# The low part of every third weight chunk from an accumulating DMA, in a two-layer fp32 decoder trunk

## The chip, the cores and the metric

The kernel runs on one core of a Trainium2 chip. The metric is the device time of one execution in microseconds (us). Three runs of the kernel before gave 1068.85, 1066.88 and 1071.05 us, median 1068.85. The core has five engines that work side by side, each through its own list of instructions in order: TensorE (PE, matmul, with its weight loads as PEld), VectorE (DVE), ScalarE (ACT), GpSimd (POOL) and SyncE (SP, which here only issues DMAs). DMAs run on 16 DMA engines that all queues share.

## The reference

One sequence of 512 tokens, width 1024, all in float32, goes through two layers. Layer 0 mixes tokens with sliding-window attention, layer 1 with a chunked spatial gating unit (SGU); each mixer is followed by a SwiGLU feed-forward (FFN) of inner width 2816. Every weight matrix is used once.

```python
def swiglu(h, w_gate_up, w_down):
    gu = h @ w_gate_up
    return (jax.nn.silu(gu[..., :D_FF]) * gu[..., D_FF:]) @ w_down

def chunked_sgu(h, w_in, ln_g, ln_b, w_spatial, b_spatial, w_out):
    z = jax.nn.gelu(h @ w_in)
    u, v = z[..., :SGU_WIDTH], z[..., SGU_WIDTH:]
    v = layernorm(v, ln_g, ln_b)
    ...
    mixed = jnp.einsum('gts,bnsgd->bntgd', ws, vg) + b_spatial.T[None, None, :, :, None]
    return (u * mixed) @ w_out          # reshapes left out

# every layer:
x += rmsnorm(mixer(rmsnorm(x)));  x += rmsnorm(swiglu(rmsnorm(x)))
```

## The kernel before, in words

**Products.** A float32 product is made from three products of a shorter type, fp32r: each operand is held as a high part (the value copied to fp32r) and a low part (the value minus its high part), and `mm3` issues high·high, high·low and low·high into one accumulator. For activations the parts are `hh`/`hl` (normed input), `ga`/`gb` (FFN inner), `rt`/`ga` (SGU output); for weights they are `wh`/`wl`.

**Weight stream.** The weights lie in memory as 1408 blocks of 128x128 in the order of their use, grouped in 176 chunks of 8 blocks (128 x 1024 floats, 512 KB). Chunks 0 to 19 belong to attention, 20 to 85 to the first FFN, 86 to 109 to the SGU (86 to 89 and 92 to 95 its `v` half, 90, 91 and 96 to 101 its `u` half, 102 to 109 its output projection), 110 to 175 to the second FFN. `fetch()` issues a chunk's load on SP into one of two `raw` buffers (line 232). `split()` then makes the parts: ACT copies `raw` into `wh` (line 255), and the inner generator `low()` has DVE subtract, `wl = raw - wh` (line 251; for chunks 0 and 1 POOL does it, line 248). Behind the subtraction `low()` calls `fetch()` for the chunk two further on, which takes the same `raw` buffer. `wh` and `wl` take one slot each of a pool of 17 slots, and a slot comes free when TensorE has used the chunk's last block. Five to eight split chunks wait ahead of TensorE in long matmul stretches.

**Order of the work.** Nothing is reordered by hand: the program that writes the kernel keeps an estimated clock for each engine (`now` for TensorE, `busy["v"]` for DVE, `busy["a"]` for ACT, `busy["d"]` for loads), advances it with every instruction it writes, and holds side chains (`Side`: norms, evacuations, splits) each with a due time. Whenever a clock passes a due time, the chain's next step is written. `split_idle()` decides when the next chunk's split is written, from the estimated idle time of DVE and ACT and a table `PLAN` per stage; `blk()` makes TensorE's order wait, at writing time, for `chunks[c][3]`, the estimated end of the chunk's low part. So the order of instructions on every engine follows from the estimates, and what they are for one instruction moves others. On the chip only the order and the data dependences count.

**Norms between stages.** A token tile's norm needs squares on ACT (line 368), a short DVE chain for the reciprocal root (`rstd`, lines 351 to 374), a scaled copy of `x` (`m`, ACT line 412 and DVE line 415), transposes on TensorE into `aux` (line 446), and evacuations into `hh` (ACT, line 459) and `hl` (DVE, line 463). Tiles 0 and 1 go together, and 2 and 3. While the norm of tiles 2 and 3 runs, TensorE works on the columns of tiles 0 and 1 of the next stage (256-column matmuls).

Of the kernel before, what the change touches and what calls it, by code (L numbers as in the profile page):

```python
# [6 lines left out]
F32 = mybir.dt.float32  # L7
I32 = mybir.dt.int32
F32R = mybir.dt.float32r
AF = mybir.ActivationFunctionType  # L10
ALU = mybir.AluOpType
PSUM = bass.MemoryType.PSUM

P = 128
# [8 lines left out]
CB = 8  # L23
# [8 lines left out]
NRAW = 2  # L32
PLAN = [(10.0, 0.0, 1.2, (), (2,)), (6.0, 0.8, 0.0, (3,), (1, 2)), (2.0, 0.3, 1.2, (2, 3), (2,)), (8.0, 0.8, 1.2, (2, 3), (2,)), (6.0, 0.3, 1.2, (2, 3), (2,)), (5.0, 0.3, 1.6, (2, 3), (2, 3)), (10.0, 0.3, 1.2, (2, 3), (2, 3)), (6.0, 0.3, 1.2, (2, 3), (2,))]
LAT = 0.1
DLAT = 1.7
X_0 = 4.0
RS = (0.27406385, -4.2420223, 5.2654107, -0.90349173, 1.7067959)
# [17 lines left out]
GU0 = WO1 + 32  # L55
# [8 lines left out]


def uses(i):
    """How many products of a 128 x 128 block the tensor engine makes with different token tiles."""
    if i < Q0 or WO0 <= i < GU0 or SO0 <= i < GU1:
        return 4
    if SV0 <= i < SO0:  # L70
        return 4 if i < SU0 or SV1 <= i < SU1 else 2 if i < SV1 else 1
    if i < WO0:
        return 1
    b = i - GU0 if i < SV0 else i - GU1
    f, b = divmod(b, 3 * HJ * KT)
    if b >= 2 * HJ * KT:
        return 4
    return 2 if f == 0 and b < 3 * 2 * KT else 1
# [3 lines left out]
def trunk_kernel(ctx, tc, x_t, w, cols, rows, ws_t, consts, out):  # L82
    nc = tc.nc
# [7 lines left out]
    wp = pool("wp", NW)  # L91
# [7 lines left out]
    def nm(s):  # L99
        cnt[0] += 1  # L100
        return f"{s}_{cnt[0]}"
# [21 lines left out]
    cols2 = [slice(0, S), slice(S, D)]  # L123
    full = slice(0, S)

    # ---- order of issue: every engine runs in the order of this trace; a clock per engine estimates
    # ---- when work is done, and a side chain joins the trace when its next step can run
    now = [0.0]
    busy = {"v": 0.0, "a": 0.0, "d": 0.0, "p": 0.0}
    sides = []  # L130

    def V(n, ready, fixed=0.07):
        busy["v"] = max(busy["v"], ready) + fixed + n * 0.00104
        return busy["v"] + LAT

    def A(n, ready, fixed=0.09):
        busy["a"] = max(busy["a"], ready) + fixed + n * 0.00084
        return busy["a"] + LAT

# [19 lines left out]
            elif not split_idle():  # L159
                return  # L160

    # the tensor engine runs at half its clock until it has been busy for a while
    zero = tp.tile([P, 4 * S], F32, tag="p", name="zero", bufs=NP)[:, 0:128].bitcast(mybir.dt.bfloat16)
    nc.vector.memset(zero[:], 0.0)
    idle_ps = [None]
# [19 lines left out]
            if not f():  # L185
                pass_time(max(now[0] + 0.01, first().due))

    # slots whose last use is traced by a side chain
    slots = {"rt": 3, "t": NT, "acc": 6}

    def take(tag):
# [20 lines left out]
        mm(ps, ah, bl, False, False)  # L212
        mm(ps, al, bh, False, stop)

# [1 line left out]
    NCH = NBLK // CB  # L216
    raws, chunks = {}, {}
    used, cur, hold, pace = [0], [0], [0.0], [5.1]
# [17 lines left out]
    def split():  # L236
        c = len(chunks)
        fetch()
        raw, ready = raws[c]
        assert used[0] + 2 <= NW  # L240
        used[0] += 2
        wh = wp.tile([P, CB * P], F32R, tag="w", name=nm("wh"))
        wl = wp.tile([P, CB * P], F32R, tag="w", name=nm("wl"))

        def low(f):
            yield f
            if c in POOL_LOW:
                nc.gpsimd.tensor_tensor(wl[:], raw[:], wh[:].bitcast(F32), ALU.subtract)
                chunks[c][3] = f + 2.4
            else:  # L250
                nc.vector.tensor_tensor(wl[:], raw[:], wh[:].bitcast(F32), ALU.subtract)  # L251
                chunks[c][3] = V(CB * P, f)
            fetch(chunks[c][3])

        nc.scalar.activation(wh[:], raw[:], AF.Copy)  # L255
        f = A(CB * P, ready)
        chunks[c] = [wh, wl, None, None, f]
        chunks[c][2] = Side(low(f), f)
# [49 lines left out]
    def drop(n=1):  # L308
        used[0] -= n

# [1 line left out]
    xs = [xp.tile([P, D], F32, tag=f"x{k}", name=f"x{k}") for k in range(NB)]  # L312
    c_cols = cp.tile([P, 42], F32, name="c_cols")
    c_msk = cp.tile([P, 384], F32, name="c_msk")
# [27 lines left out]
    def b_qk(i):  # L342
        return c_cols[:, 32 + i:33 + i]

# [1 line left out]
    def rsqrt(us, ready, scale=1.0):  # L346
        ws = [[small(1, i) for i in ("vt", "vy", "vz", "vq", "vw")] for _ in us]
        rs = [sp.tile([P, 8], F32, tag="rc", name=nm("rc"), bufs=8)[:, 0:1] for _ in us]
# [171 lines left out]
                self.nx.add(t, s2, self.m, f)  # L520

    class LastTok(Tok):
        """The last token tile: nothing runs behind it, so its second half comes in two pieces."""
        parts = (slice(0, S), slice(S, S + 256), slice(S + 256, D))

        def __init__(self, t, m, g1, spare_m):
# [65 lines left out]
            if free:  # L592
                give("acc")

# [1 line left out]
    def ffn(base, nx_in, g1o, nx_out):  # L596
        def evac_gu(g, jj, pg, pu, hf):
            n = hf.stop - hf.start
# [100 lines left out]
                    toks[t].add(i + 1, ps, V(256, now[0] + 0.2))  # L699
            drop()  # L700

# [1 line left out]
    def attention(nx_in, g1o, nx_out):  # L703
        v4 = wp.tile([P, NB, 256], F32, tag="w", name=nm("vt"))
        vt = [v4[:, t] for t in range(NB)]
# [4 lines left out]
        ready = {}  # L710
# [105 lines left out]
        def softmax(u, g2, st, es, sm, f):  # L816
# [13 lines left out]
            V(4, f, 0.15)  # L830
            f = busy["v"] + LAT
            for j in js[NA:]:
# [8 lines left out]
        def values(u):  # L841
# [11 lines left out]
            fs = {}  # L853

            def pv(kt):
                """Both heads of a pair, side by side in the columns of the array."""
                f = max(fs[2 * kt], fs[2 * kt + 1])
                if f > now[0]:
                    yield f
                for i in range(2):  # L860
                    o = (2 * pr + i) * 64
                    nc.tensor.matmul(po[i * 64:i * 64 + 64, :], vt[n - nkt + 1 + kt][:, o:o + 64], todo[2 * kt + i],  # L862
                                     start=kt == 0, stop=kt == nkt - 1)
                    now[0] += 0.02 if i else 0.86
                    give("t")
# [19 lines left out]
            f = A(S, now[0] + 0.2)  # L885
# [14 lines left out]
        order = []  # L900
# [64 lines left out]
            hold[0] = now[0] + (NB - 1 - t) * 8 * 0.65  # L965
        drop(2)

# [1 line left out]
    def sgu(nx_in, g1o, nx_out):  # L969
        ln_g, ln_b, bsp = row_tile(0), row_tile(1), row_tile(2)  # L970
        h = hsrc(nx_in)
# [279 lines left out]
```

## Time and profile before

| | us |
|---|---|
| runs | 1068.85, 1066.88, 1071.05 (median 1068.85) |
| span of the profiled execution | 1067.4 |
| median less span | 1.45 |
| PE busy | 1047.9 (98% of the span) |
| DVE busy | 524.6 (49%) |
| ACT busy | 439.8 (41%) |
| POOL busy | 23.6 (2%) |
| mean granted TensorE clock | 0.997 of full speed (2.4 GHz) |

The trace comes from one profiled execution, whose span runs from its first to its last instruction; a busy share is an average over stages, so what counts at a place is read from the rows of that place. A row of the timeline has the start, the duration, engine, line, operation, destination `<-` sources and, in brackets, how long the engine stood idle before it and what ended that. `xN` is a run of N equal instructions put in one row, with their time together. Matmuls overlap, so a matmul's duration is longer than the distance to the next one's start; the distance is what it costs.

### The profile page before, as it was taken

How to read it: one execution, taken by the hardware profiler on the slowest of the kernel's cores; microseconds unless marked ns; L12 is line 12 of the kernel's file. 1: busy time of each engine (PE TensorE's matmuls, PEld its weight loads, DVE VectorE, ACT ScalarE, POOL GpSimd, SP SyncE). 2: the span in 40 equal slices, each digit the busy share in tenths (PEclk: the TensorE clock that was granted, in tenths of full speed). 3: DMA queues.
4: the chain of work that ended last, by engine and by line, in shares of the span. 5: the costliest groups of instructions: out<-in, count | busy, mean ns of one | idle time of the engine just before them, and what ended most of it. 6: DMA issues, size and time to landing. Idle time of an engine off the chain costs nothing.

```text
span 1067.4 us, 13460 instructions
## 1 busy us (share of the span) xinstructions
PE 1047.9 (98%) x5288; PEld 873.5 (82%) x5288; DVE 524.6 (49%) x1103; ACT 439.8 (41%) x792; POOL 23.6 (2%) x21
## 2 busy tenths in 40 slices
PE   7999998999999999999999999999999999999997
PEld 6877766988888888888888888899888888888886
DVE  7588879743332233332474867584333223333335
ACT  6589776632322223232255343573223222232210
POOL 2000001000000000000000000100000000000000
PEclk9999999999999999999999999999999999999999
DMA  5322201332222222224132232033222222222202
GB/s 206 126 79 80 80 21 60 134 125 98 99 99 98 99 99 99 98 84 136 60 117 101 80 125 103 30 119 147 92 98 99 99 99 99 99 99 99 99 0 79
DMA packets 29263, 103.00 MB, mean 96 GB/s; under 512 B 3280, under 2 KB 3808, under 8 KB 29200
## 3 DMA queue, kind: packets, MB, share of 16 engines
q1 hardware_dynamic: 28512, 101.00, 26.1%
q8 instruction: 41, 0.67, 0.2%
q10 hardware_dynamic: 576, 0.92, 0.2%
q0 software_dynamic: 112, 0.23, 0.2%
q14 instruction: 22, 0.18, 0.0%
HBM read 100.04 MB, written 2.10 MB: 96 GB/s over the span
## 4 chain that ended last, share of the span: by engine, by line
PE 92%; DVE 4%; DMA 2%; ACT 1%; issue 1%; SPq 0%; DVEq 0%; ACTq 0%
PE acc L204 88%; PE acc L862 1%; PE aux L870 1%; DMA x<-x_t 1%; DMA raw<-w 1%; DVE wl L251 1%; PE aux L446 1%; DVE x L509 0%; DVE u L374 0%; DVE hl L463 0%; DVE m L963 0%; DVE p L833 0%; DVE m L1141 0%; PE acc L446 0%; DVE vt L353 0%
## 5 line engine op out<-in xcount | busy, mean ns | idle before, releaser
L251 DVE TENSOR_TENSOR wl<-raw,wh 128x1024 fp32r<-128x1024 f32 x174 | 213.5, 1228 | 415.9 <-PE acc L204 341.4
L204 PE MATMUL acc<-hh,wh 128*128 128x512 f32 (+1 forms) x960 | 351.7, 366 | 0.0
L204 PE MATMUL acc<-hl,wh 128*128 128x512 f32 (+1 forms) x960 | 349.9, 364 | 0.6 <-DVE hl L463 0.6
L204 PE MATMUL acc<-hh,wl 128*128 128x512 f32 (+1 forms) x960 | 349.7, 364 | 0.0
L255 ACT ACTIVATE wh<-raw 128x1024 fp32r<-128x1024 f32 x176 | 185.8, 1057 | 221.9 <-PE acc L204 187.8
L204 PE MATMUL acc<-wh,ga 128*128 128x512 f32 (+1 forms) x736 | 234.6, 389 | 3.0 <-DVE ga L889 3.0
L204 PEld LDWEIGHTS acc<-hl,wh 128*128 128x128 f32 x960 | 181.1, 189 | 29.4 <-DVE hl L463 1.0
L204 PEld LDWEIGHTS acc<-hh,wh 128*128 128x128 f32 x960 | 181.1, 189 | 28.9
L204 PEld LDWEIGHTS acc<-hh,wl 128*128 128x128 f32 x960 | 181.0, 189 | 28.9
L204 PEld LDWEIGHTS acc<-wh,ga 128*128 128x128 f32 x736 | 137.2, 188 | 35.2 <-DVE ga L889 3.4
L204 PE MATMUL acc<-wl,ga 128*128 128x512 f32 (+1 forms) x368 | 141.7, 385 | 0.0
L601 ACT ACTIVATE t<-acc 128x512 f32<-128x512 f32 (+1 forms) x50 | 27.2, 544 | 146.9 <-PE acc L204 146.9
L204 PEld LDWEIGHTS acc<-wl,ga 128*128 128x128 f32 x368 | 69.2, 188 | 12.7
L204 PE MATMUL acc<-wh,gb 128*128 128x512 f32 (+1 forms) x198 | 61.9, 383 | 0.0
L611 ACT ACTIVATE ga<-t 128x512 fp32r<-128x512 f32 (+1 forms) x38 | 21.4, 563 | 53.2 <-DVE t L607 53.1
L204 PEld LDWEIGHTS acc<-wh,gb 128*128 128x128 f32 x198 | 36.9, 188 | 7.2
L490 POOL TENSOR_TENSOR m<-m,row 128x512 f32<-128x512 f32 x12 | 16.9, 1409 | 1020.4 <-ACT acc L368 1020.4
L204 PE MATMUL acc<-wl,gb 128*128 128x512 f32 (+1 forms) x99 | 37.9, 383 | 0.0
L368 ACT ACTIVATE acc<-m 128x512 f32<-128x512 f32 x30 | 17.9, 598 | 45.4 <-DVE m L676 42.1
L204 PE MATMUL acc<-wh,hh 128*128 128x512 f32 (+1 forms) x96 | 34.6, 363 | 1.5 <-ACT wh L255 1.5
L204 PE MATMUL acc<-wl,hh 128*128 128x512 f32 (+1 forms) x96 | 34.0, 364 | 0.0
L204 PE MATMUL acc<-wh,hl 128*128 128x512 f32 (+1 forms) x96 | 33.9, 355 | 0.0
(117 smaller groups left out, 838.9 us busy)
## 6 DMA issues: line engine op xcount, KB each, us to landing
raw<-w SPq DMA_DIRECT2D x176, 512.0 KB, 3.4
row<-rows SPq DMA_DIRECT2D x8, 512.0 KB, 4.6
x<-x_t SPq DMA_DIRECT2D x4, 512.0 KB, 5.6
out<-x SPq DMA_DIRECT2D x4, 256.0 KB, 2.1
out<-x ACTq DMA_DIRECT2D x3, 256.0 KB, 2.1
cs<-consts SPq DMA_DIRECT2D x1, 512.0 KB, 4.7
t<-ws_t SPq DMA_DIRECT2D x2, 256.0 KB, 4.5
c_row<-rows POOLq DMA_DIRECT2D x1, 136.0 KB, 7.3
```

What stands on the lines that cost most here:

```text
L204: nc.tensor.matmul(ps, a, b, start=start, stop=stop)
L251: nc.vector.tensor_tensor(wl[:], raw[:], wh[:].bitcast(F32), ALU.subtract)
L255: nc.scalar.activation(wh[:], raw[:], AF.Copy)
L368: nc.scalar.activation(junk, src, AF.Square, accum_out=s[:, c:c + 1])
L446: nc.tensor.transpose(dst, self.src[t][k // 4][:, (k % 4) * P:(k % 4 + 1) * P], ident)
L490: nc.gpsimd.tensor_tensor(self.m[c][:], self.m[c][:], self.g1[:, cols2[c]], ALU.mult)
L601: nc.scalar.activation(t1[:, hf], pg[:, hf], AF.Silu)
L611: nc.scalar.activation(g[0][jj][:, hf], t1[:, hf], AF.Copy)
L862: nc.tensor.matmul(po[i * 64:i * 64 + 64, :], vt[n - nkt + 1 + kt][:, o:o + 64], todo[2 * kt + i], start=kt == 0, stop=kt == nkt - 1)
L870: nc.tensor.transpose(pT[:, g * P:(g + 1) * P], u.pt[:, g, i, kt * P:(kt + 1) * P], ident)
```

## The change

Behind attention, from chunk 28 on, the chunks whose number is a multiple of 3 (30, 33, ..., 174: 49 chunks) get their low part in another way. ACT writes `wh` as before, and then a second copy with scale -1, `-wh`, into the slot of the low part (now called `wlq`). An accumulating DMA issued by POOL then adds `raw` onto it: -wh + raw. DVE has no part in these chunks. The load of the chunk two further on takes the same `raw` buffer, and so comes behind the accumulating DMA. The estimate of that DMA's length, `DMA_LOW`, is 6.0 us. Comments and docstrings are gone too; they are not shown here. Line numbers behind the new code are 21 higher than before (`wl` on DVE is line 272, the plain `wh` 276, the squares 389, the scaled copy 433, the transposes 467).

```diff
+DMA_LOW = 6.0
...
+    def by_dma(c):
+        return c * CB >= GU0 + 64 and c % 3 == 0
+
     NCH = NBLK // CB
...
         wh = wp.tile([P, CB * P], F32R, tag="w", name=nm("wh"))
+        if by_dma(c):
+            wl = wp.tile([P, CB * P], F32R, tag="w", name=nm("wlq"))
+
+            def low_dma(f):
+                yield f
+                nc.scalar.activation(wl[:], wh[:].bitcast(F32), AF.Copy, scale=-1.0)
+                f = A(CB * P, f)
+                yield f
+                nc.gpsimd.dma_start(wl[:], raw[:], accum_op=ALU.add)
+                chunks[c][3] = f + DMA_LOW
+                fetch(chunks[c][3])
+
+            nc.scalar.activation(wh[:], raw[:], AF.Copy)
+            f = A(CB * P, ready)
+            chunks[c] = [wh, wl, None, None, f]
+            chunks[c][2] = Side(low_dma(f), f)
+            return
         wl = wp.tile([P, CB * P], F32R, tag="w", name=nm("wl"))
```

DVE has 49 instructions fewer, ACT 49 more, POOL 49 DMAs more; PE and SP have as many as before. Because the estimates differ, the order moves as well, at the changes of stage above all. Three places follow; names end in a number that the program counts up, and `...` stands for rows left out.

The first is TensorE at the start of the SGU, where the transposes of the last two token tiles of FFN 0 (`aux<-c_id,m`) are mixed into the 256-column matmuls on chunk 90 (`wh_789`, `wl_790`; in the change `wlq_790`) and chunk 91 (`wh_802`). Before:

```order
L204 MATMUL acc_822_4856<-hh_747_4610,wh_789_4751 128x256
L204 MATMUL acc_822_4856<-hl_755_4618,wh_789_4751 128x256
L204 MATMUL acc_822_4856<-hh_747_4610,wl_790_4752 128x256
...
L204 MATMUL acc_822_4856<-hh_754_4617,wl_790_4752 128x256
L204 MATMUL acc_825_4886<-hh_747_4610,wh_802_4791 128x256
...
L204 MATMUL acc_825_4886<-hh_748_4611,wl_803_4792 128x256
L446 MATMUL aux_826_4893<-c_id_96,m_541_3139 128x128
L446 MATMUL aux_826_4893<-c_id_96,m_543_3141 128x128
```

In the change:

```order
L205 MATMUL acc_820_4874<-hh_747_4630,wh_789_4771 128x256
L205 MATMUL acc_820_4874<-hl_755_4639,wh_789_4771 128x256
L205 MATMUL acc_820_4874<-hh_747_4630,wlq_790_4772 128x256
L467 MATMUL aux_821_4878<-c_id_96,m_541_3146 128x128
L467 MATMUL aux_821_4878<-c_id_96,m_543_3148 128x128
...
L205 MATMUL acc_820_4874<-hh_748_4631,wh_789_4771 128x256
```

The first transpose stood behind 30 of these matmuls (24 on chunk 90, 6 on chunk 91) and now stands behind 3, so it moved ahead of 27.

The second is ACT at the same place: the splits of chunks 90 and 91, the squares of tile 3 (`m_543,s2<-x3`) and the scaled copies that feed those transposes. Before:

```order
L255 ACTIVATE wh_789_4751<-raw_776_4685 128x1024
L999 ACT_TABLE_LOAD
L999 ACTIVATE m_800_4782<-acc_785_4721 128x512
L255 ACTIVATE wh_802_4791<-raw_788_4731 128x1024
L368 ACTIVATE m_543_3141,s2_799_4779<-x3_93 128x512
L368 ACTIVATE m_544_3142,s2_799_4779<-x3_93 128x512
L255 ACTIVATE wh_805_4814<-raw_791_4762 128x1024
L412 ACTIVATE m_541_3139<-x2_92,rc_819_4834 128x512
```

In the change:

```order
L259 ACTIVATE wh_789_4771<-raw_776_4705 128x1024
L252 ACTIVATE wlq_790_4772<-wh_789_4771 128x1024
L1020 ACT_TABLE_LOAD
L1020 ACTIVATE m_799_4800<-acc_785_4741 128x512
L276 ACTIVATE wh_802_4812<-raw_788_4751 128x1024
L389 ACTIVATE m_543_3148,s2_798_4797<-x3_93 128x512
L389 ACTIVATE m_544_3149,s2_798_4797<-x3_93 128x512
L433 ACTIVATE m_541_3146<-x2_92,rc_817_4846 128x512
```

The negated copy stands behind chunk 90's `wh`; the squares still stand behind chunk 91's `wh` (`wh_802`), and chunk 92's `wh` (`wh_805`) no longer stands ahead of the scaled copies.

The third is ACT at the end of the SGU's mixing. `rt` and `ga` from line 1075 (1096 in the change) are the high parts of the SGU's gated output, and the next evacuation is line 1107 (1128). Before, where `wh_928` and `wh_931` are chunks 106 and 107 and `wh_972` is chunk 108:

```order
L255 ACTIVATE wh_928_5509<-raw_923_5481 128x1024
L255 ACTIVATE wh_931_5524<-raw_927_5495 128x1024
L1039 ACTIVATE p_912_5412<-acc_926_5490 128x512
L1075 ACTIVATE rt_941_5536<-p_824_4884 128x512
...
L1075 ACTIVATE ga_944_5539<-p_912_5412 128x512 x4
L255 ACTIVATE wh_972_5731<-raw_930_5519 128x1024
L255 ACTIVATE wh_975_5743<-raw_947_5556 128x1024
```

In the change, where `wh_966`, `wh_969` and `wh_972` are chunks 106, 107 and 108:

```order
L1060 ACTIVATE p_912_5435<-acc_921_5506 128x512
L1096 ACTIVATE rt_935_5550<-p_828_4935 128x512
...
L1096 ACTIVATE ga_938_5553<-p_912_5435 128x512 x4
L276 ACTIVATE wh_966_5742<-raw_924_5529 128x1024
L276 ACTIVATE wh_969_5754<-raw_941_5570 128x1024
L259 ACTIVATE wh_972_5775<-raw_968_5746 128x1024
L252 ACTIVATE wlq_973_5776<-wh_972_5775 128x1024
```

Chunks 106 and 107 are split behind the `rt` and `ga` copies instead of ahead of them, and chunk 108, which is one of the 49, follows them.

## Rows read from the trace of the kernel before

**Rows 1.** Page, busy time of each engine (share of span, instructions)
```profile
PE 1047.9 (98%) x5288; PEld 873.5 (82%) x5288; DVE 524.6 (49%) x1103; ACT 439.8 (41%) x792; POOL 23.6 (2%) x21
```

**Rows 2.** Page, chain of work that ended last: share of the span by engine
```profile
PE 92%; DVE 4%; DMA 2%; ACT 1%; issue 1%; SPq 0%; DVEq 0%; ACTq 0%
```

**Rows 3.** Busy time by stretch: stretch, its length, then each engine's busy time
```profile
560.00:715.00 155.00, 154.25 (x861) 134.29 (x860) 106.42 (x245) 78.78 (x138) 6.19 (x4) 1.00 0.26 93
715.00:1040.00 325.00, 325.00 (x1507) 272.24 (x1506) 108.00 (x122) 95.06 (x126) 1.53 (x1) 1.00 0.26 94
```

**Rows 4.** Page, costliest groups: busy, mean ns, idle before; the subtraction
```profile
L251 DVE TENSOR_TENSOR wl<-raw,wh 128x1024 fp32r<-128x1024 f32 x174 | 213.5, 1228 | 415.9 <-PE acc L204 341.4
```

**Rows 5.** View of line 251: who waited for it (us, times)
```profile
  PEld acc L204: 1.6, 2
```

**Rows 6.** Timeline around chunk 147 in the second FFN
```profile
854.09 0.33 SPq L232 DMA_DIRECT2D raw<-w  x1
...
858.50 1.07 ACT L255 ACTIVATE wh<-raw 128x1024 fp32r<-128x1024 f32 x1 [4.37 <-PE acc L204]
...
858.28 1.23 DVE L251 TENSOR_TENSOR wl<-raw,wh 128x1024 fp32r<-128x1024 f32 x1 [4.22 <-PE acc L204]
863.72 1.22 DVE L251 TENSOR_TENSOR wl<-raw,wh 128x1024 fp32r<-128x1024 f32 x1 [4.21 <-PE acc L204]
...
902.22 0.39 PE L204 MATMUL acc<-hh,wl 128*128 128x512 f32 x1
```

**Rows 7.** Page, DMA queues and DMA issues: KB each, median us to landing
```profile
q1 hardware_dynamic: 28512, 101.00, 26.1%
...
raw<-w SPq DMA_DIRECT2D x176, 512.0 KB, 3.4
...
c_id<-consts POOLq DMA_DIRECT2D x1, 64.0 KB, 4.7
```

**Rows 8.** Timeline of POOL at the start: a DMA that it issues
```profile
1.95 0.54 POOL L320 DMA_DIRECT2D c_cols<-cols  x1
```

**Rows 9.** Timeline of SP, ACT and PE at the start of the SGU
```profile
551.97 0.33 SPq L232 DMA_DIRECT2D raw<-w  x1
...
552.98 1.06 ACT L255 ACTIVATE wh<-raw 128x1024 fp32r<-128x1024 f32 x1 [1.41 <-DMA raw<-w]
...
560.41 1.06 ACT L255 ACTIVATE wh<-raw 128x1024 fp32r<-128x1024 f32 x1 [3.02 <-DMA raw<-w]
...
564.13 1.34 ACT L412 ACTIVATE m<-x,rc 128x512 f32<-128x512 f32 x2 [0.49 <-DVE rc L363]
...
560.69 0.28 PE L204 MATMUL acc<-hh,wh 128*128 128x256 f32 x1
...
564.16 0.28 PE L204 MATMUL acc<-hh,wl 128*128 128x256 f32 x1
564.91 0.33 PE L446 MATMUL aux<-c_id,m 128*128 128x128 f32 x1 [0.47 <-ACT m L412]
```

**Rows 10.** Timeline of ACT, DVE and PE around chunks 106 to 109
```profile
639.01 1.06 ACT L255 ACTIVATE wh<-raw 128x1024 fp32r<-128x1024 f32 x1 [1.39 <-DMA raw<-w]
...
656.88 2.00 ACT L255 ACTIVATE wh<-raw 128x1024 fp32r<-128x1024 f32 x2
...
658.03 2.35 DVE L251 TENSOR_TENSOR wl<-raw,wh 128x1024 fp32r<-128x1024 f32 x2
...
667.82 0.39 PE L204 MATMUL acc<-wl,ga 128*128 128x512 f32 x1
```

**Rows 11.** Timeline of SP, ACT, DVE and PE around chunks 112 to 114
```profile
699.86 0.33 SPq L232 DMA_DIRECT2D raw<-w  x1
...
697.52 1.05 ACT L255 ACTIVATE wh<-raw 128x1024 fp32r<-128x1024 f32 x1
...
704.94 1.22 DVE L251 TENSOR_TENSOR wl<-raw,wh 128x1024 fp32r<-128x1024 f32 x1
...
708.57 0.28 PE L204 MATMUL acc<-hh,wl 128*128 128x256 f32 x1
```

## The prediction, made before the change was run

> **What bounds the kernel now.** I read the busy times first, then the chain of waits, then the busy times by stretch. TensorE is busy in 98% of the span, DVE in 49%, ACT in 41% [rows 1], and the chain that ended last lies on TensorE for 92% and on DVE for 4% [rows 2]. From 715 to 1040 us TensorE has no idle time at all, and in the stretch around the SGU it lacks 0.75 us of 155 [rows 3]. Outside the start and the tail, which the change does not touch, there is then hardly a microsecond to gain: about 0.75 us by busy time, about 2 us if I allow for matmul records being drawn longer than their pitch. The operation that the change removes is not what TensorE waits for: of all 174 subtractions on DVE two were waited for, 1.6 us together [rows 5], and DVE's own idle time in front of them, 341.4 us of 415.9, ends when TensorE frees a slot [rows 4]. So the question is only where the new path is late.
>
> **What is removed and added, in the long stretches.** DVE loses 49 x 1.228 = 60 us [rows 4], ACT gains 49 negated copies at the 1.07 us of a high-part copy [rows 6], 52 us. Neither is on the path: in the second FFN DVE is busy 108 of 325 us and ACT 95 [rows 3]. A chunk feeds 24 matmuls of 512 columns and is used up in 863.72 - 858.28 = 5.44 us [rows 6]. Chunk 147's low part was done at 864.94, its first use at 902.22: a lead of 37.3 us. That lead is the cover.
>
> What the new path costs in it hangs on one number that the trace does not show: the time L from the end of the negated copy to the landing of the accumulated data. The nearest rows: a load of the same 512 KB lands after 3.4 us, a 64 KB DMA issued by POOL after 4.7 us [rows 7], and POOL spends 0.54 us on issuing one [rows 8]. The queue with the loads holds all 16 DMA engines for 26.1% of 1067.4 us with 101 MB [rows 7], that is 192.6 transfers of 512 KB (101/0.524), so 1.45 us each; the fixed part of a load is 3.4 - 1.45 = 1.95. An accumulating DMA has to read two operands and write one, so I give it one to two transfer times more. L = 0.54 + 1.95 + 1.45 + (1.45 to 2.9) = 5.4 to 6.8; I take 6.5, at the dear end, because the one small DMA on POOL's queue took 4.7. Bounds: 3.4, if it behaves as a load does; and 12, from the load that was issued at 551.97 among other transfers and whose copy began at 560.41, 8.44 us [rows 9], plus two transfers and the issue.
>
> The Trainium skill (Collectives: The Full Stack, on why ReduceScatter is half of AllGather) says that an add in the DMA engines costs not arithmetic but a second source read for each write. By that alone one transfer time is added and L is 5.4; no row here shows an accumulating DMA.
>
> In steady state three chunks are used in 3 x 5.44 = 16.3 us. One of the two raw buffers is held through the load (3.4), two copies (2.1) and L, and the load behind it in SP's queue waits for that too. Refilling three chunks therefore takes about L + 6.5 us, less than 16.3 as long as L is under 9.8. Up to there the lead of 37.3 us stays and this part costs nothing. ACT now waits for TensorE's slot in place of DVE, some 4.2 us once in three chunks [rows 6]; behind it in ACT's list stand evacuations of accumulators, for whose banks TensorE could wait. But ACT waits as long (4.37 us) in front of its copies before, and TensorE loses nothing by it (325.00 of 325.00 us, [rows 3]). Bounds: nothing, and 4.2 us for each of a few evacuations that follow a negated copy closely; I take nothing.
>
> **What is moved: the start of the SGU.** TensorE's transposes of tiles 2 and 3 move ahead of 27 matmuls of 256 columns. The 30 matmuls from 560.69 to 564.16 have a pitch of 3.47/29 = 0.12 us [rows 9], so TensorE arrives 27 x 0.12 = 3.24 us earlier. Their input does not come earlier: the scaled copy at 564.13 follows the root, which follows tile 3's squares on ACT, and these stand behind chunk 91's high-part copy in both orders. That copy began at 560.41, when its load landed, and the idle time in front of it (3.02 us) ended by that DMA [rows 9]. DVE's missing subtraction gives nothing back here, as the load sets the time. TensorE's wait in front of the transposes, which was 0.47 us and another short one, becomes 3.24 us longer, and the 27 matmuls do not vanish, they only come later: +3.24 us. Moreover the accumulating DMA of chunk 90 starts at about 556 us, while chunk 91's load is under way: between nothing and its two transfers (2.9) are added to that landing; I take 1.3. This place: +4.5 us (3.2 to 6.1). Chunk 90's own low part would be needed at 560.9, two pitches behind 560.69, and its copy began at 552.98 [rows 9], so the negated copy ends at about 555.1; with L = 6.5 it lands at 561.6, 0.7 us late, but TensorE then only spends a part of the wait at the transposes before them. The chunk's cover is gone at L of about 10.
>
> **Chunk 108.** Before, the copies of chunks 106 and 107 came ahead of the gating copies (the latter at 639.01), so chunk 108's load had landed long before its own copy at 656.88; its subtraction ended 658.03 + 1.18 = 659.2 and its first use was at 667.82 [rows 10]: 8.6 us of slack. Now chunk 106 is split behind the gating copies. One subtraction (1.2 us) leaves the DVE chain ahead, so I let chunk 106's copy begin about 1.1 us before 656.88, at 655.8, and its subtraction end at about 658.2. Only then may chunk 108's load start; it lands 3.4 later (661.6), the two copies take it to 663.7, L to 663.7 + 6.5 = 670.2. That is 2.4 us behind 667.82, and TensorE has nothing else in its list: +2.4 us, in general L - 4.1, from 0 (L under 4.1) to 7.9 (L = 12).
>
> **Chunk 114.** The load was issued at 699.86, the subtraction ended at 706.16, the use was at 708.57 [rows 11]: only 2.4 us of slack. Here the order helps: chunk 112's copy moves from 697.52 to about 691.8, its subtraction ends near 695.2, the load lands at 698.7, the negated copy ends behind another chunk's at about 701.2. With L it is there at 707.7: no stall, above L = 7.4 one of L - 7.4. The transposes of this change of stage move ahead of 6 to 12 short matmuls each; I put 0.3 us on these and all else.
>
> **Sum.** 4.5 + 2.4 + 0.3 = +7.2 us on the profiled 1067.4, so 1074.6; the median of the runs lies 1.45 above the profiled span, which gives 1076.0. By L: 4 gives 1073.7, 5 gives 1074.5, 8 gives 1078, 10 gives 1082, 12 gives 1086 (chunks 108 and 114 with 7.9 and 4.6). By the page's rule alone (L = 5.4) it would be 1074.9.
>
> **Rivals.** *Hidden.* L is near 4, or TensorE's wait at the transposes is shorter than I think, since the chain in front of them loses a subtraction. For it: 37 us of lead nearly everywhere and idle DVE and ACT. Against it: the load's landing in [rows 9] doesn't hang on DVE. The time: 1068.85 + 2 to 5, so 1071 to 1074.
>
> *The other side: faster.* DVE's subtractions delay the norm chains at the changes of stage, and without them a chain's root is ready earlier by one or two subtractions. That decides if TensorE's remaining gaps there (0.75 to 2 us) lie behind such a chain and no other place loses. Price: at most 2 us, so 1067; the new order uses this up before it can show, since it puts the transposes earlier than their input.
>
> *Starvation.* L above 9.8, so that refilling three chunks takes longer than using them; the two raw buffers and SP's queue then decide. Every 16.3 us the lead shrinks by L - 9.8, over about 19 triples in each FFN: with L = 12 the loss is 42 us against a lead of 37, so some 5 us of stall in each, and 1086 becomes 1096; with L = 15 it is 99 - 37, about 60 us for each FFN, and over 1200. Against it: a load through a crowd took 8.44 us, and beside one accumulating DMA there are only two loads.
>
> *Held-up issue.* DVE's work could hold up the issue on POOL. If each issue had to wait for two DVE operations as long as a subtraction (2.45 us, [rows 4]), L would be 9, and the time 1068.85 + 4.5 + 4.9 + 1.6 + 0.3 = 1080. DVE is busy in a third of the FFN stretches [rows 3], so most such delays would meet the lead there and not TensorE. The Trainium skill (SBUF — State Buffer, the trap "DVE blocks DMA") says that a DMA from GpSimd's queue gets its descriptors in software, and that these cannot be written while DVE runs one of its two-port modes; its example goes from 620 to 3100 ns, about as much as the two operations. No run here shows it.
>
> *The change doesn't do what it says.* If the DMA replaced the slot's content instead of adding, no time would show it; if the accumulating DMA were not one transfer but many small ones, L would be far above 12, with the time of starvation.
>
> **How the numbers follow.** What a measurement of this kernel can tell from no change is about 0.5%, 5.3 us: 1063.5 to 1074.2. My forecast (L of 5 to 8, the two stalls as worked out) has 0.54; hidden 0.25; L of 8 to 12, the held-up issue among it, 0.10; starvation and not as said 0.06; the faster side 0.05. The forecast's own lower edge lies at the bound, so 0.08 of it counts as "same"; of the faster side 0.02, as it is worked out at 2 us at most, and 0.03 for its price being too small. Within 0.5%: 0.25 + 0.08 + 0.02 = 0.35; slower by over 0.5%: 0.46 + 0.10 + 0.06 = 0.62; faster by over 0.5%: 0.03. The range of 8 in 10 goes from 1070, where hidden cases with both stalls small lie, to 1090, above L = 12 without much erosion.
>
> **What would show it right or wrong.** Right: in the profile of the changed kernel TensorE waits 3 to 5 us in front of the transposes (line 467) at about 561 us, and about 2 us on chunk 108's low part some 108 us later; the landing of the accumulating DMAs is 5.4 to 6.8 us behind the negated copies; in the long stretches TensorE has no idle time and DVE is 60 us less busy. Wrong: a landing beyond 9.8 us with waits spread over both FFNs; a TensorE wait at another change of stage; or no wait at the transposes, which would mean that tile 3's squares did not hang on chunk 91's load.

## The result, and the profile after

The changed kernel takes 1074.76 us (median of 11 runs, 1070.58 to 1076.65) against 1069.17 us of the kernel before (11 runs beside it, 1066.88 to 1071.05). The ratio is 1.005, 95% interval 1.0035 to 1.0064: slower by half a per cent. (Ratios here and below are those on record; they can differ by up to 0.0007 from the quotient of the medians.) The forecast was 1076.0 us, range 1070 to 1090.

The page of the changed kernel: busy time by engine, the share of the chain, two DMA queues, and the median time from issue to landing. They answer to [rows 1, 2, 7].

```profile
PE 1050.6 (98%) x5288; PEld 875.7 (82%) x5288; DVE 467.8 (44%) x1054; ACT 485.5 (45%) x841; POOL 65.9 (6%) x70
...
q1 hardware_dynamic: 28512, 101.00, 27.7%
q0 software_dynamic: 7168, 25.92, 12.9%
...
PE 89%; DVE 5%; DMA 2%; ACT 1%; issue 1%; SPq 0%; DVEq 0%; POOLq 0%; ACTq 0%
...
raw<-w SPq DMA_DIRECT2D x176, 512.0 KB, 3.5
wlq<-raw POOLq DMA_DIRECT2D x49, 512.0 KB, 4.6
```

DVE is 56.8 us less busy and ACT 45.7 us more. The accumulating DMAs hold all 16 engines for 12.9% of 1073.8 us, 2.83 us each; a load (27.7%, 192.6 transfers) holds them for 1.54 us here, against 1.45 before; that is not the DMAs' doing, since the order alone, below, has 1.56 without any of them. An accumulating DMA costs 1.8 loads of the engines' time, and lands 4.6 us after its issue.

The costliest groups of the new path, on the same page (busy, mean ns, idle before), answer to [rows 4]:

```profile
L272 DVE TENSOR_TENSOR wl<-raw,wh 128x1024 fp32r<-128x1024 f32 x125 | 152.8, 1223 | 364.1 <-PE acc L205 232.7
...
L252 ACT ACTIVATE wlq<-wh 128x1024 fp32r<-128x1024 f32 x49 | 52.0, 1061 | 82.6 <-PE acc L205 81.9
L255 POOL DMA_DIRECT2D wlq<-raw x49 | 42.5, 867 | 754.8 <-ACT wlq L252 707.9
```

Where the time went is seen best by TensorE's own instructions: there are 5288 in both traces, in nearly the same order (the filled kernel's 28 added ones are left out), so the start of the n-th matmul after less that before gives a running balance. I call this the path. The table has, worked out so from each trace, what the path gains (+ is later) in a stretch, for the changed kernel and for the experiments below. The first column is the start of the program, which the change doesn't touch: it varies by up to 1.6 us from one execution to the next, and has to be left out.

| kernel | up to 540 us | SGU start | SGU gating (chunk 108) | FFN 1 start | to the end, all |
|---|---|---|---|---|---|
| the change | -0.26 | +5.33 | +1.58 | -0.18 | +6.47 |
| order alone | -0.17 | +5.27 | 0 | -0.19 | +4.91 |
| order alone, filled | -1.61 | +2.40 | 0 | -0.19 | +0.60 |
| old order, DMAs | +0.24 | +3.00 | +9.62 | +4.10 | +16.96 |
| not 90 and 108 | -0.63 | -1.07 | 0 | +1.94 | +0.24 |
| squares first | -0.68 | -0.13 | +1.63 | -0.18 | +0.64 |
| before, squares first | -0.12 | -1.20 | 0 | -0.02 | -1.34 |
| DMAs inside FFNs only | +1.16 | -1.20 | 0 | -0.01 | -0.05 |

So all of it is lost at two places, the two that the prediction named, and nothing in the long stretches. First the SGU start in the changed kernel: the timeline of SP, ACT, POOL and TensorE, to be held against [rows 9].

```profile
551.71 0.33 SPq L236 DMA_DIRECT2D raw<-w  x1
...
554.55 1.06 ACT L252 ACTIVATE wlq<-wh 128x1024 fp32r<-128x1024 f32 x1
560.52 1.06 ACT L276 ACTIVATE wh<-raw 128x1024 fp32r<-128x1024 f32 x1 [3.00 <-DMA raw<-w]
564.18 1.34 ACT L433 ACTIVATE m<-x,rc 128x512 f32<-128x512 f32 x2 [1.37 <-DVE rc L384]
...
556.02 0.88 POOL L255 DMA_DIRECT2D wlq<-raw  x1 [12.69 <-ACT wlq L252]
...
560.54 0.28 PE L205 MATMUL acc<-hl,wh 128*128 128x256 f32 x1
562.97 0.58 PE L205 MATMUL acc<-hh,wlq 128*128 128x256 f32 x1 [2.15 <-DMA wlq<-raw]
564.95 1.52 PE L467 MATMUL aux<-c_id,m 128*128 128x128 f32 x4 [1.40 <-ACT m L433]
566.12 0.56 PE L205 MATMUL acc<-hh,wh 128*128 128x256 f32 x1
```

TensorE comes to chunk 90's low part at 560.66, waits 2.15 us for it, does one matmul, and waits 1.40 us more for the transposes' input. That input is there at 564.95; before, at 564.91 [rows 9]. Behind the wait the matmuls are slower: 0.56 us for one that takes 0.36 before. The busy times by stretch show why; after the times of PE, PEld, DVE, ACT and POOL each row has the granted clock as a share of 2.4 GHz:

```profile
562.00:564.00 2.00, 0.58 (x1) 0.29 (x1) 2.00 (x16) 0.81 (x4) 0.00 (x0) 0.70 0.12 12
564.00:566.00 2.00, 0.91 (x3) 0.62 (x4) 1.06 (x5) 1.82 (x3) 0.00 (x0) 0.50 0.90 252
566.00:568.00 2.00, 2.00 (x12) 2.00 (x11) 0.62 (x2) 0.84 (x2) 0.00 (x0) 0.50 0.66 268
568.00:572.00 4.00, 4.00 (x30) 4.00 (x30) 2.46 (x5) 2.76 (x6) 0.00 (x0) 0.80 0.00 0
```

During the wait the granted clock fell to its lower level, 1.2 GHz, and stayed there until about 569.6 us. From the first transpose to the 60th TensorE instruction behind it takes 9.40 us here, and 7.57 where the clock did not fall (the filled kernel below): 1.83 us. So 5.33 = 3.50 of waiting + 1.83 of clock in this execution.

Then chunk 108: ACT, POOL and TensorE of the changed kernel, against [rows 10].

```profile
661.34 2.00 ACT L276 ACTIVATE wh<-raw 128x1024 fp32r<-128x1024 f32 x2
667.17 1.06 ACT L259 ACTIVATE wh<-raw 128x1024 fp32r<-128x1024 f32 x1 [3.84 <-DMA raw<-w]
668.27 1.06 ACT L252 ACTIVATE wlq<-wh 128x1024 fp32r<-128x1024 f32 x1
...
669.73 0.86 POOL L255 DMA_DIRECT2D wlq<-raw  x1 [24.50 <-ACT wlq L252]
...
674.34 0.50 PE L205 MATMUL acc<-wlq,ga 128*128 128x512 f32 x1 [1.29 <-DMA wlq<-raw]
```

Chunk 106 is split at 661.34, behind the gating copies; chunk 108's load may only start then, and ACT waits 3.84 us for it. The negated copy ends at 669.33, the data are there just before 674.34: L, the time from the negated copy's end to the landing, is 5.0 us, of which 0.4 pass before POOL issues and 4.6 from there to the landing. TensorE waits 1.29 us (the path shows 1.58; the records of matmuls are longer than their pitch, and the first one behind the wait is slower).

### The profile page after: what moved, and what is told of

Same layout as the page of the kernel before. It is cut to its first block, busy times and chain, and to the rows that moved or that the text cites. A ratio compares the mean times of both kernels' runs of the same rounds, so it can differ in the third digit from the quotient of the medians.

```text
span 1073.8 us, 13564 instructions
## 1 busy us (share of the span) xinstructions
PE 1050.6 (98%) x5288; PEld 875.7 (82%) x5288; DVE 467.8 (44%) x1054; ACT 485.5 (45%) x841; POOL 65.9 (6%) x70
## 3 DMA queue, kind: packets, MB, share of 16 engines
q1 hardware_dynamic: 28512, 101.00, 27.7%
q0 software_dynamic: 7168, 25.92, 12.9%
## 4 chain that ended last, share of the span: by engine, by line
PE 89%; DVE 5%; DMA 2%; ACT 1%; issue 1%; SPq 0%; DVEq 0%; POOLq 0%; ACTq 0%
PE acc L205 86%; DMA raw<-w 1%; PE acc L883 1%; PE aux L891 1%; DVE wl L272 1%; DMA x<-x_t 1%; PE aux L467 1%; DMA wlq<-raw 0%; DVE x L530 0%; DVE u L395 0%; DVE p L1093 0%; DVE hl L484 0%; DVE m L1110 0%; DVE m L984 0%; DVE p L854 0%
## 5 line engine op out<-in xcount | busy, mean ns | idle before, releaser
L272 DVE TENSOR_TENSOR wl<-raw,wh 128x1024 fp32r<-128x1024 f32 x125 | 152.8, 1223 | 364.1 <-PE acc L205 232.7
L205 PE MATMUL acc<-hh,wl 128*128 128x512 f32 (+1 forms) x712 | 258.3, 363 | 0.0
L205 PEld LDWEIGHTS acc<-hh,wl 128*128 128x128 f32 x712 | 134.3, 189 | 21.0
L205 PE MATMUL acc<-hh,wlq 128*128 128x512 f32 (+1 forms) x248 | 92.1, 372 | 2.1 <-DMA wlq<-raw 2.1
L205 PE MATMUL acc<-wl,ga 128*128 128x512 f32 (+1 forms) x237 | 91.3, 385 | 0.0
L252 ACT ACTIVATE wlq<-wh 128x1024 fp32r<-128x1024 f32 x49 | 52.0, 1061 | 82.6 <-PE acc L205 81.9
L255 POOL DMA_DIRECT2D wlq<-raw x49 | 42.5, 867 | 754.8 <-ACT wlq L252 707.9
L628 DVE TENSOR_TENSOR t<-t,acc 128x512 f32<-128x512 f32 (+1 forms) x50 | 31.0, 620 | 99.7 <-ACT t L622 53.6
L205 PEld LDWEIGHTS acc<-hh,wlq 128*128 128x128 f32 x248 | 47.4, 191 | 10.1 <-DMA wlq<-raw 2.3
L205 PE MATMUL acc<-wlq,ga 128*128 128x512 f32 (+1 forms) x131 | 50.5, 385 | 1.3 <-DMA wlq<-raw 1.3
```

What stands on the lines that cost most here:

```text
L205: nc.tensor.matmul(ps, a, b, start=start, stop=stop)
L252: nc.scalar.activation(wl[:], wh[:].bitcast(F32), AF.Copy, scale=-1.0)
L255: nc.gpsimd.dma_start(wl[:], raw[:], accum_op=ALU.add)
L628: nc.vector.tensor_tensor(t1[:, hf], t1[:, hf], pu[:, hf], ALU.mult)
```

## The experiments

**The order alone.** TensorE, ACT and SP get the order of the changed kernel, and the estimates stay as they are, but DVE subtracts again.

```diff
             def low_dma(f):
                 yield f
-                nc.scalar.activation(wl[:], wh[:].bitcast(F32), AF.Copy, scale=-1.0)
                 f = A(CB * P, f)
                 yield f
-                nc.gpsimd.dma_start(wl[:], raw[:], accum_op=ALU.add)
+                nc.vector.tensor_tensor(wl[:], raw[:], wh[:].bitcast(F32), ALU.subtract)
                 chunks[c][3] = f + DMA_LOW
```

> The changed kernel's order on TensorE, ACT and SP, but the 49 low parts are made by DVE's subtraction again and the negated copies are left out. Theory (the moved order): TensorE still waits about 4 us in front of the transposes at the start of the SGU, the granted clock falls there as in the changed kernel, TensorE's path there is 4.8 to 5.3 us longer than before, nothing at chunk 108: 1074 us (1073 to 1075). Rival (the accumulating DMAs' late landing is the cause): nothing is left of the loss, 1069 us (1068 to 1070).

Measured: 1072.63 us (5 runs) against 1069.24, ratio 1.0036 (1.0024 to 1.0049). The path loses 5.27 us at the SGU start, as much as with the DMAs, and nothing at chunk 108. TensorE's timeline there:

```profile
560.75 0.28 PE L205 MATMUL acc<-hh,wlq 128*128 128x256 f32 x1
564.24 1.51 PE L466 MATMUL aux<-c_id,m 128*128 128x128 f32 x4 [3.21 <-ACT m L432]
```

And the busy times behind it, with the granted clock at 0.50:

```profile
564.00:566.00 2.00, 1.62 (x7) 1.33 (x7) 0.29 (x1) 1.49 (x4) 0.00 (x0) 0.50 0.39 156
```

One wait of 3.21 us for the transposes' input stands where there were two. So the 2.15 us that the changed kernel's trace puts down to the accumulating DMA were a part of a wait that would have been there without it: the transposes' input, which hangs on chunk 91's load, comes later still. That the two paths agree to 0.06 us is in part chance. Chunk 91's load landed 7.9 us after its issue in this trace and 8.8 in the changed kernel's, so the wait is 2.70 us here and 3.50 there, while the clock costs 2.57 and 1.83 (next experiment). Set to the 8.4 us of the kernel before, both waits come to 3.1 to 3.2 us. By median the order alone costs 3.4 us of the change's 5.6 (by path 5.27 of 6.9); the theory's 1074 (from 1073) was 1.4 too high, the rival's 1069 is excluded.

**The same, with the wait filled.** 28 transposes of the identity matrix, whose result nothing uses, ahead of the first awaited transpose.

```diff
                     ps = aux()
+                if self.gv == 2 and 2 in ts and k0 == 0:
+                    for _ in range(28):
+                        nc.tensor.transpose(ps[:, 0:P], ident, ident)
                 for k in range(k0, k0 + kn):
```

> The kernel with the changed order and DVE's subtractions, and 28 transposes of the identity matrix, which nothing uses, ahead of the first awaited transpose at the start of the SGU, so that TensorE works in place of waiting. Theory (of the 5.3 us lost there 3.2 to 3.5 are the wait and some 1.8 the halved clock behind it): the awaited transposes start as late as without the filling, the granted clock stays at full speed, and TensorE's path there is 3.4 us longer than before: 1071.2 us (1070.2 to 1072). Rival (the clock has no part, it is all wait): 1072.6 us, path 5.3 us longer, as without the filling.

Measured: 1071.62 us (9 runs), ratio 1.0025 (1.0014 to 1.0036). TensorE's timeline at the place:

```profile
559.44 3.22 PE L461 MATMUL aux<-c_id 128*128 128x128 f32 x28
562.50 0.33 PE L469 MATMUL aux<-c_id,m 128*128 128x128 f32 x1
```

The busy times behind it, with the granted clock:

```profile
564.00:566.00 2.00, 2.00 (x20) 2.00 (x18) 1.44 (x4) 2.00 (x5) 0.00 (x0) 1.00 0.00 0
```

The clock stays at full speed in this execution, and the path loses 2.40 in place of 5.27 us. Of these 2.87 us, 0.33 come from chunk 91's load, which landed that much sooner in this execution; the clock's part is 10.14 - 7.57 = 2.57 us over the same 60 instructions. By medians the two kernels differ by 1.0 us, less than the theory's 1.4, with intervals that overlap. The two traces show the clock's part; the run times alone would not. The traces are also of extreme runs, the quickest of the nine here (1069.73) and the slowest of the five without the filling (1074.05), so that the filling keeps the clock in every execution is not shown.

**The old order, with the DMAs.** The negated copy and the DMA are written in the step in which DVE's subtraction was, and the estimate is that of DVE. TensorE's order is then that of the kernel before, row for row.

```diff
                 nc.scalar.activation(wl[:], wh[:].bitcast(F32), AF.Copy, scale=-1.0)
-                f = A(CB * P, f)
-                yield f
                 nc.gpsimd.dma_start(wl[:], raw[:], accum_op=ALU.add)
-                chunks[c][3] = f + DMA_LOW
+                chunks[c][3] = V(CB * P, f)
```

> The old kernel's order on TensorE, DVE and SP, and the 49 low parts by negated copy and accumulating DMA. Theory (the moved order): at the start of the SGU chunk 90's low part lands near 562.5 against a need at 560.9, about 2 us, of which the old wait of 1.3 us at the transposes is given back, so +0.7 us; chunk 108 has its slack back; chunk 114 is late by about 2 us since its load is late again: 1072 us (1070 to 1073). Rival (late landings alone): 1074.5 us or more, since all the DMAs of the changed kernel are in it.

Measured: 1086.06 us (4 runs), ratio 1.0156 (1.0143 to 1.017). The theory was far too low; the rival's "or more" holds the number, but neither had the mechanism, which costs 9.62 us at the gating. ACT, POOL and TensorE there:

```profile
645.13 1.05 ACT L252 ACTIVATE wlq<-wh 128x1024 fp32r<-128x1024 f32 x1
647.71 1.06 ACT L274 ACTIVATE wh<-raw 128x1024 fp32r<-128x1024 f32 x1 [1.53 <-DMA raw<-w]
655.16 1.06 ACT L274 ACTIVATE wh<-raw 128x1024 fp32r<-128x1024 f32 x1 [6.39 <-DMA raw<-w]
...
646.58 0.86 POOL L253 DMA_DIRECT2D wlq<-raw  x1 [10.62 <-PE acc L205]
...
656.76 5.38 PE L205 MATMUL acc<-ws,ga 128*128 128x128 f32 x24 [4.52 <-ACT p L1058]
```

The busy times behind it, with the granted clock at 0.50 again:

```profile
656.00:660.00 4.00, 3.24 (x15) 3.25 (x16) 3.75 (x6) 1.33 (x3) 0.00 (x0) 0.50 0.50 182
```

In the old order chunk 107's high-part copy stands in ACT's list ahead of an evacuation that TensorE waits for (`p`). Its load takes the raw buffer of chunk 105, one of the 49, and may start only when that chunk's DMA, issued at 646.58, has landed. ACT stands idle for 6.39 us at that copy, TensorE for 4.52 behind it, and then runs at the lower clock. At the FFN 1 start chunk 114 is late by 2.3 us (4.10 by path, the clock included). At the SGU start this order loses 3.00, and the same mechanism has the greater part of it. ACT and TensorE there:

```profile
566.42 1.06 ACT L274 ACTIVATE wh<-raw 128x1024 fp32r<-128x1024 f32 x1 [4.09 <-DMA raw<-w]
...
562.52 0.39 PE L205 MATMUL acc<-hh,wlq 128*128 128x256 f32 x1 [1.19 <-DMA wlq<-raw]
...
568.15 0.33 PE L465 MATMUL aux<-c_id,m 128*128 128x128 f32 x1 [2.02 <-ACT m L431]
```

TensorE waits 1.19 us for chunk 90's landing, since the transposes no longer hide it. But chunk 92's load takes chunk 90's raw buffer and is issued only behind that landing, at 562.52; ACT waits 4.09 us for it at chunk 92's copy, which in this order stands ahead of the scaled copies, and the transposes wait 2.02 us for those. So the order that the change's estimates bring about is not only where time is lost; with that DMA latency the old order is far worse.

**Without chunks 90 and 108.**

```diff
-        return c * CB >= GU0 + 64 and c % 3 == 0
+        return c * CB >= GU0 + 64 and c % 3 == 0 and c not in (90, 108)
```

> As the changed kernel, but chunks 90 and 108 keep DVE's subtraction (47 accumulating DMAs); the order at the start of the SGU is then that of before. Theory (two places make the loss): 1069.3 us (1068.3 to 1070.3), and no wait of TensorE on an accumulating DMA. Rival (a general cost of the 49 DMAs, the negated copies, or the traffic): the loss stays near 5 us, 1073 to 1075.

Measured: 1070.63 us (11 runs), ratio 1.0013 (1.0004 to 1.0022). The loss at both places is gone, and with it most of the whole: the rival, a general cost of the DMAs, falls. The median is 0.3 us above the theory's range, and the trace is of the quickest of the eleven runs (1069.37). Two things are off. At the SGU start the path gained 1.07 us; chunk 91's load landed 7.4 us after its issue here and 8.4 before, so that is the execution, not the kernel. And 1.94 us are lost at 704 to 709 us, at transposes that this order puts earlier; only 0.9 us of it are shown as waits (0.5 for their input, 0.4 for an accumulating DMA, where the theory had none), the rest I did not pursue.

**The squares first.** ACT takes tile 3's squares ahead of chunk 91's copy, by keeping that chunk's split back until they are written.

```diff
         if c not in raws or raws[c][1] > now[0]:
             return False
+        if c == 91 and not squared[0]:
+            return False
...
                 self.nx.add(t, s2, self.m, f)
+                if t == 3 and self.nx.gv == 2:
+                    squared[0] = True
```

In the changed kernel:

> The changed kernel, but ACT takes the squares of tile 3 ahead of chunk 91's high-part copy, and so does not wait for chunk 91's load first; the transposes stand two or three matmuls from where the changed kernel has them. Theory (at the start of the SGU the transposes' input decides, and the landing of chunk 90's accumulating DMA is hidden in that wait): the transposes no longer wait, chunk 90's landing at about 563 becomes the only wait, 2.2 us, and TensorE's path there is 1 to 2.5 us longer than before in place of 5.3: 1071.5 us (1070.5 to 1073). Rival (chunk 90's landing sets the end): 1074.5 us as the changed kernel.

Measured: 1072.02 us (12 runs), ratio 1.003 (1.002 to 1.004), in place of 1.005. The path loses nothing at the SGU start (-0.13; chunk 91's load came 1.3 us sooner here than in the changed kernel's trace, so in a like execution it might be +1.1), and 1.63 at chunk 108 as before:

```profile
555.70 0.88 POOL L255 DMA_DIRECT2D wlq<-raw  x1 [12.79 <-ACT wlq L252]
...
560.56 0.33 PE L469 MATMUL aux<-c_id,m 128*128 128x128 f32 x1 [0.39 <-ACT m L435]
561.80 0.28 PE L205 MATMUL acc<-hh,wlq 128*128 128x256 f32 x1
```

TensorE's waits from 540 to 760 us (in total, times, longest):

```profile
PE acc L205 <- DMA wlq<-raw: 1.3, 1, 1.3
```

The last row is the only wait on an accumulating DMA between 540 and 760 us, chunk 108's. Chunk 90's landed 5.6 us after its issue, at 561.26, where the changed kernel's took 6.9. The trace is of one of the quicker runs (1069.77): its path is 0.64 us longer than before to the end, the median 3.1, so the trace shows less of a loss than most runs had.

In the kernel before, without any accumulating DMA:

> The kernel before, but ACT takes the squares of tile 3 ahead of chunk 91's high-part copy; no accumulating DMA. Theory (the squares stand behind a load that they don't need): TensorE's waits at the transposes, 1.4 us, go: path 1.2 us shorter, 1068.0 us (1067.3 to 1069). Rival (DVE's chain or tile 3 itself is late anyway): no change, 1069.2 us.

Measured: 1067.86 us (11 runs) against 1068.92, ratio 0.9987 (0.9978 to 0.9996): the fastest of all, though by little. Its chunk 91 was copied as late as ever, and yet TensorE goes into the transposes without a wait:

```profile
560.62 1.06 ACT L255 ACTIVATE wh<-raw 128x1024 fp32r<-128x1024 f32 x1 [1.58 <-DMA raw<-w]
...
563.32 0.28 PE L204 MATMUL acc<-hh,wl 128*128 128x256 f32 x1
563.44 0.60 PE L448 MATMUL aux<-c_id,m 128*128 128x128 f32 x4
```

So the squares did hang on a load that they don't need, as the prediction had it.

**The DMAs inside the FFNs only.** The kernel with the squares first, and the 39 accumulating DMAs of chunks 30 to 84 and 117 to 174; TensorE's order is that of the kernel just above.

```diff
-        return c * CB >= GU0 + 64 and c % 3 == 0
+        return c * CB >= GU0 + 64 and c % 3 == 0 and not 86 <= c <= 116
```

> As the kernel before with tile 3's squares ahead of chunk 91's copy (TensorE's order is the same), and every third chunk from 30 to 84 and from 117 to 174 by negated copy and accumulating DMA, 39 of them, all inside the FFNs. Theory (inside the FFNs the lead hides them): the same time as without them, 1068.0 us (1067.3 to 1069), no wait of TensorE on such a DMA. Rival (each DMA costs TensorE something, by traffic or by ACT's time): over 1070 us.

Measured: 1067.74 us (11 runs; 1067.86 without the DMAs), ratio to the kernel before 0.9996 (0.9986 to 1.0006). Behind the program's start the path is the same as without them to 0.02 us. Where the lead is long, 39 subtractions on DVE and 39 accumulating DMAs are worth the same to the end: nothing.

**Every chunk of the FFNs.**

```diff
-        return c * CB >= GU0 + 64 and c % 3 == 0
+        return c * CB >= GU0 + 64 and (c % 3 == 0 or c < 86 or c >= 114)
```

> Every chunk of both FFNs from 30 to 85 and 114 to 175 by negated copy and accumulating DMA, elsewhere every third. Theory (refill bound by a raw buffer held through load, two copies and landing): a buffer is held 3.5 + 2.1 + 5.1 = 10.7 us or more for each second chunk, and used up in 10.9, so that with the crowded queues it falls short by about 1 us for each chunk; the lead of 37 us is used up behind some 40 chunks, and TensorE waits 10 to 30 us in each FFN: 1090 to 1130 us. Rival (the lead covers it all): TensorE has no idle time in the long stretches, 1074 to 1080 us.

Measured: 1182.29 us (one run). The landing times on its page:

```profile
raw<-w SPq DMA_DIRECT2D x176, 512.0 KB, 4.0
wlq<-raw POOLq DMA_DIRECT2D x129, 512.0 KB, 5.2
```

TensorE's waits (in total, times, longest):

```profile
PE acc L205 <- DMA wlq<-raw: 80.4, 46, 4.5
```

Two copies on ACT from the same raw buffer, one round apart:

```profile
1004.51 1.06 ACT L259 ACTIVATE wh<-raw 128x1024 fp32r<-128x1024 f32 x1 [6.95 <-DMA raw<-w]
1018.07 1.06 ACT L259 ACTIVATE wh<-raw 128x1024 fp32r<-128x1024 f32 x1 [7.49 <-DMA raw<-w]
```

And the second FFN by busy time, with the DMA share behind the clock:

```profile
760.00:1040.00 280.00, 260.43 (x1199) 211.89 (x1198) 26.75 (x45) 115.98 (x138) 38.12 (x44) 0.99 0.69 163
```

The mechanism was right and the size too small: a buffer comes round in 13.56 us for two chunks where TensorE uses them in 10.9, so 1.3 us are lost for each chunk, not 1. The waits come to 80.4 us of the 113 that the path loses; the granted clock has a mean of 0.972 in this run, and how much of the rest it explains I did not sort out. The DMA engines are busy for 0.69 only, so the row of steps on one buffer is the limit, as far as the rows show, and not the traffic.

## Why the prediction was right, and where it was off

- *What bounds the kernel.* Right. TensorE has no idle time from 720 to 1040 us in the changed kernel either (320.00 of 320.00 us), and taking 57 us from DVE gained nothing there.
- *L.* 6.5 us was taken, bounds 3.4 and 12, the estimate 5.4 to 6.8; measured 5.0 in the median of the 49 and 7.3 at most, at chunk 90. The step that added 1.45 to 2.9 us for the second operand was the one that was too dear: the engines are held for 1.29 us longer than by a load (2.83 against 1.54), and the landing comes 1.1 us later than a load's. In this the trace agrees with the Trainium skill (Collectives: The Full Stack, on why ReduceScatter is half of AllGather), which prices an add at a second source read; I estimate that as one more transfer, 1.54 us by the load, where 1.29 was measured. By that rule the sum stood at 1074.9, nearer than mine.
- *SGU start.* 4.5 predicted, 5.33 measured, by partly other terms. The 3.24 us of transposes moved ahead of their input were there (3.50 in this execution; 3.1 to 3.2 here, in the order alone and in the filled kernel once each one's load is set to the 8.4 us of before). The 1.3 us for chunk 90's DMA in the way of chunk 91's load were not: that load landed 8.8 us after its issue, 8.4 before, and between 7.4 and 8.8 in the experiments, 8.8 once without any accumulating DMA near; the three traces with chunk 90's DMA have a mean of 8.1, the six without it 8.0. In its place stands a term that the prediction had not: TensorE's clock fell during the wait, 1.83 us. That the place came out near its 4.5 is partly luck: a term that was missing made up for one that was not there.
- *Chunk 90 itself.* Predicted 0.7 us late, measured 2.2 us, hidden by the same wait as was said; the order alone shows that.
- *Chunk 108.* 2.4 predicted, 1.58 measured. The chain came step by step as worked out; with L = 5.0 its formula gives 0.9. Of the other 0.7, some 0.6 lie at the copies: the negated copy ended at 669.33, less the path's 5.07 by then 664.26, where I had 663.7.
- *Chunk 114.* No stall, as predicted; in the old order it is late, which is what the forecast's earlier copy of chunk 112 had avoided.
- *The signs.* A wait of 3 to 5 us in front of the transposes: the changed kernel's trace names only 1.40 there and 2.15 at the matmul ahead of them, the order alone 3.21 there. About 2 us on chunk 108: 1.29. A landing 5.4 to 6.8 us behind the negated copies: 5.0. DVE 60 us less busy: 56.8.
- *The sum.* 7.2 predicted, 6.4 by the profiled spans (1073.8 against 1067.4), 5.6 by medians. The SGU start came out 0.8 us dearer and chunk 108 0.8 cheaper; that the two misses cancel is luck.
- *The rivals.* *Starvation* did not come at one chunk in three, and came at all of them. *Held-up issue:* the 49 issues took 0.85 to 0.93 us and the landings nearly all 4.5 to 5.1, so it is not seen here: 32 issues stood beside a DVE that was idle or nearly so and 15 beside one that was busy for over half of the issue, with medians of 4.56 and 4.59 us to the landing. The rule of the Trainium skill (SBUF — State Buffer, the trap "DVE blocks DMA") is not contradicted by that, since I did not sort out which DVE operations ran beside an issue.

What stays open: the runs of the changed kernel spread over 6 us. The clock has a part in that. The two quickest runs (1070.58 and 1070.71) have a mean granted clock of 0.999, which leaves room for only some 2 us at half the clock in the whole run (0.001 x 1069 us, doubled); the 6.8 us of the trace above, 562.8 to 569.6, cannot have come in them. The five from 1075.09 on have 0.991 to 0.994. So the clock does not fall at this place in every execution, even without the filling. Why it does in one and not in another, and how much chunk 91's landing adds to the spread, is not shown: there is one trace of each kernel.

## What to carry to other kernels

Work taken from an engine with slack is worth nothing, and the new path has to be judged by its latency where the lead is short: at one chunk in three every loss was at a change of stage. Where a written order follows from estimates, compare the orders first; in the changed kernel the moved transposes cost 5.3 us and the DMAs 1.6, while the same DMAs in the old order cost 17. A wait that a trace names (2.15 us on the DMA) can be covered by a later one. Price a wait of TensorE of 3 us or so with the clock that it may lose behind it, and look for instructions that stand behind a load they don't need.

## What the runs showed that I had not expected

- In two traces waits of TensorE of 3.2 and 3.6 us in all went with a fall of the granted clock to 1.2 GHz, which lasted some 5 to 6 us behind the wait and cost 2.6 and 1.8 us more; in the one trace with the wait filled by transposes that nothing uses it stayed at 2.4 GHz. By their mean clocks, two runs of the changed kernel did not have this fall either.
- A raw buffer held 5 us longer blocks more than its own chunk: in the old order one late load held ACT for 6.39 us and TensorE behind it, with its clock, for 9.6, and another, chunk 92's, held ACT for 4.09 us and TensorE for 2.02.
- The same 512 KB load among two broadcast loads landed 7.4 to 8.8 us after its issue from one execution to the next.
